# A layer-norm chain with a shorter reciprocal square root, its normalization on ScalarE, and a raised scheduling priority

## The chip, the core and the metric

One core of a Trainium2 chip runs the whole program. The metric is the device time of one execution in microseconds (us). Engines are named as in the profile: PE is TensorE (matmuls and PE transposes), DVE is VectorE, ACT is ScalarE, POOL is GpSimd, SP issues the DMAs. Each engine works through its own list of instructions in order.

## What is computed

256 tokens of width 1024 pass through 12 sublayers (4 layers of feed-forward, mixer, feed-forward; the mixers are latent attention, differential attention, a Mamba-2 scan and latent attention again), each closed by a residual sum and a layer norm, and then through a second block of three sublayers with RMS norms. What the change touches is the closing of a sublayer:

```python
def _layernorm(x, g, b):
    xf = x.astype(jnp.float32)
    mu = jnp.mean(xf, axis=-1, keepdims=True)
    var = jnp.mean(jnp.square(xf - mu), axis=-1, keepdims=True)
    return ((xf - mu) * lax.rsqrt(var + LN_EPS) * g + b).astype(x.dtype)

def _rmsnorm(x, g):
    xf = x.astype(jnp.float32)
    return (xf * lax.rsqrt(jnp.mean(xf * xf, axis=-1, keepdims=True) + RMS_EPS) * g).astype(x.dtype)

def _swiglu(h, w_in, w_out):
    gate, up = jnp.split(h @ w_in, 2, axis=-1)
    return (jax.nn.silu(gate) * up) @ w_out

def _sublayer(x, fn, mod_j, g, b, weight):
    shift, scale, gate = mod_j[:, 0, None, :], mod_j[:, 1, None, :], mod_j[:, 2, None, :]
    y = fn(x * (1 + scale) + shift)
    return _layernorm(DEEPNORM_ALPHA * x + weight * gate * y, g, b)
```

Weights and activations are float32.

## The kernel before, in words

**Tiles.** The tokens are two tiles of 128 rows, t = 0 and t = 1. A product of float32 operands is made of three matmuls of rounded parts (`mm3`, lines 252 to 254): high activation by high weight, high by low, low by high. So each weight that a DMA brings in (`raw`) is split: ACT copies the high part (`whi`, line 219, 128x1024 at a time) and DVE subtracts to get the low part (`wlo`, line 222, pieces of 384, 384 and 256 columns). These splits run all the time beside the matmuls, and most of DVE's and ACT's instructions are of this kind.

**A feed-forward (FFN).** 11 blocks of the hidden width. For each block and tile `first` makes `hid` (lines 252 to 254), ACT the gate `sg` (line 613), DVE the product `ac` (line 616); `turn` transposes `ac` on PE (line 263) and splits the result into `ah` (ACT, line 625) and `al` (DVE, line 626); `second` adds to the output banks `y` with three matmuls (line 640 `whi` by `ah`, 641 `wlo` by `ah`, 642 `whi` by `al`). In PSUM, `y0q` belongs to tile 0 and `y1q` to tile 1. Near its end the steps stand in the order `O1.b T1.c F O1.c D1` after `D0`: tile 0 is closed (`D0`) while tile 1 still has blocks to do, and then tile 1 (`D1`).

**The close of a sublayer.** `post_ln` (line 521), called once for each tile of the 12 sublayers, 24 times in all: on DVE y times gate (528) and plus ALPHA times x (529) for two halves of 512, `bn_stats` (530), `bn_aggr` (532), the reciprocal root `rstd` (311 to 325, three Newton steps on a 128x1 column, with alternating lines 319 and 320), and the normalization of `r` in two halves of 512 (535). Then `halves` transposes `r` on PE in two groups of four (`tr<-k_ident,r`, line 263), ACT applies gain, bias and modulation during the evacuation (`ev`, line 285) and takes the high part (`tmp`, line 287), and DVE the low part (295). That is what the next sublayer's first matmul (`hid0t`, `pa` or `ph`) waits for. The plain output `x = r*lng + lnb` (540, 541, full width) is a `late` step that only the next close needs.

**rstd elsewhere.** 62 calls: 24 from layer norms, 30 more for a single column (RMS norms, among them `cn`, line 768, of the latent attention, and the end of the kernel, line 589), 8 for several columns, which use lines 322 to 324.

**What sets the order.** Strings such as the one quoted list the steps of a sublayer. Within it the framework's scheduler sorts each engine's instructions by priority (by default the order of writing) as their inputs are expected to be ready, and fills gaps between dependent instructions with others, so `wlo` pieces stand between the steps of a layer norm.

Of the kernel before, what the change touches and what calls it, by code (L numbers as in the profile page):

```python
# [13 lines left out]
I32 = mybir.dt.int32  # L14
AF = mybir.ActivationFunctionType
OP = mybir.AluOpType
# [15 lines left out]
WLO, ACH, WHI, NRM = 384, 1024, 1024, 512  # L32
# [131 lines left out]
class Net:  # L164
# [145 lines left out]

    def rstd(self, var, n, mul, eps):
        e = self.nc.vector
        v, h, r, t = (self.small(n, z) for z in ("rv", "rh", "rs", "rt"))
        e.tensor_scalar(v, var, mul, eps, op0=OP.mult, op1=OP.add)
        e.tensor_scalar(r.bitcast(I32), v.bitcast(I32), -0.5, 1597463007.0, op0=OP.mult, op1=OP.add)
        e.tensor_scalar(h, v, -0.5, None, op0=OP.mult)
        for _ in range(3):
            if n == 1:
                e.tensor_scalar(t, h, r, r, op0=OP.mult, op1=OP.mult)
                e.tensor_scalar(r, t, 1.5, r, op0=OP.add, op1=OP.mult)  # L320
            else:
                e.tensor_tensor(t, r, r, OP.mult)
                e.tensor_tensor(t, t, h, OP.mult)
                e.scalar_tensor_tensor(r, t, 1.5, r, OP.add, OP.mult)
        return r

    def rms_from(self, ss, n, dim, eps=RMS_EPS):
# [193 lines left out]
    def post_ln(self, t, y, k, last=False):  # L521
        nc = self.nc
        x = self.x[t]
        r = self.tmp([P, 1024], name="r")
        st = self.small(12, "st").rearrange("p (a b) -> p a b", a=2)
        for q in range(2):
            sl = slice(q * 512, (q + 1) * 512)
            nc.vector.scalar_tensor_tensor(r[:, sl], y[q], self.gweight, self.gw[:, sl], OP.mult, OP.mult)
            nc.vector.scalar_tensor_tensor(r[:, sl], x[:, sl], ALPHA, r[:, sl], OP.mult, OP.add)
            nc.vector.bn_stats(st[:, q, :], r[:, sl])  # L530
        mv = self.small(2, "mv")
        nc.vector.bn_aggr(mv, st)
        rs = self.rstd(mv[:, 1:2], 1, 1.0, LN_EPS)
        for q in range(0, 1024, NRM):
            nc.vector.tensor_scalar(r[:, q:q + NRM], r[:, q:q + NRM], mv[:, 0:1], rs, op0=OP.subtract, op1=OP.mult)
        lng, lnb, xn = self.lng, self.lnb, self.xn
        GB = self.GB.get(k)

        def gain():
            nc.vector.tensor_tensor(x, r, lng, OP.mult)  # L540
            nc.vector.tensor_tensor(x, x, lnb, OP.add)

        if last:
            return [gain]
        if k == 3 * DEPTH:
            if GB is None:
                GB = self.GB[k] = self.small(8, "G"), self.small(8, "B")
                for o, v in zip(GB, (self.lngc, self.lnbc)):
                    nc.vector.tensor_tensor(o, v[:, (k - 1) * 8:k * 8], self.g2["pre_mix_g_2"], OP.mult)

            def late():
                gain()
                ss = self.small(2, "ss")
                self.square([x[:, q * 512:(q + 1) * 512] for q in range(2)], ss)
                self.pre_rms(t, ss)
            return self.halves(r, xn, t, GB[0], GB[1]) + [late]
        self.late.append(gain)
        return self.halves(r, xn, t, GB[0], GB[1])
# [1035 lines left out]
```

## Time and profile before

| | |
|---|---|
| three runs | 2566.07, 2568.09, 2568.38 us, median 2568.09 |
| span of the profiled execution | 2567.9 us (its own time is not listed apart from the three) |
| PE busy | 2497.5 us, 97% |
| DVE busy | 2129.1 us, 83% |
| ACT busy | 1286.9 us, 50% |
| chain that ended last | PE 86%, DVE 7%, DMA 3%, ACT 2%, issue 1% |

The busy time of an engine is a sum over all its instructions, the chain follows back from the last instruction what released each step. A row of the timeline has start, duration, engine, line, operation, output and inputs, and in brackets how long the engine had been idle and who ended that. A row for several instructions of one kind carries a count (x5).

### The profile page before, as it was taken

How to read it: one execution, taken by the hardware profiler on the slowest of the kernel's cores; microseconds unless marked ns; L12 is line 12 of the kernel's file. 1: busy time of each engine (PE TensorE's matmuls, PEld its weight loads, DVE VectorE, ACT ScalarE, POOL GpSimd, SP SyncE). 2: the span in 40 equal slices, each digit the busy share in tenths (PEclk: the TensorE clock that was granted, in tenths of full speed). 3: DMA queues.
4: the chain of work that ended last, by engine and by line, in shares of the span. 5: the costliest groups of instructions: out<-in, count | busy, mean ns of one | idle time of the engine just before them, and what ended most of it. 6: DMA issues, size and time to landing. Idle time of an engine off the chain costs nothing.

```text
span 2567.9 us, 34087 instructions
## 1 busy us (share of the span) xinstructions
PE 2497.5 (97%) x12252; PEld 2065.0 (80%) x12252; DVE 2129.1 (83%) x4847; ACT 1286.9 (50%) x2005; POOL 0.2 (0%) x4
## 2 busy tenths in 40 slices
PE   7999899999999999999999999999989999999998
PEld 6788688888887788888889778887878888788887
DVE  7888988879898988898989987698898856896754
ACT  3544474444446544544566554454446544555542
POOL 0000000000000000000000000000000000000000
PEclk9999999999999999999999999999999999999999
DMA  8888457848876388688742457658845754444552
GB/s 309 308 340 306 159 194 276 309 169 300 321 267 256 123 299 320 221 299 316 270 158 99 164 202 292 252 211 324 310 166 211 275 179 175 164 157 172 200 180 80
DMA packets 92297, 599.15 MB, mean 233 GB/s; under 512 B 12768, under 2 KB 14432, under 8 KB 24672
## 3 DMA queue, kind: packets, MB, share of 16 engines
q1 hardware_dynamic: 92128, 596.98, 63.5%
q8 instruction: 96, 1.57, 0.2%
q14 instruction: 73, 0.60, 0.1%
HBM read 593.79 MB, written 3.15 MB: 232 GB/s over the span
## 4 chain that ended last, share of the span: by engine, by line
PE 86%; DVE 7%; DMA 3%; ACT 2%; issue 1%; SPq 0%; DVEq 0%; ACTq 0%
PE tr L263 4%; PE y0q L640 3%; PE y0q L642 3%; PE y0q L641 3%; PE y1q L640 3%; PE y1q L642 3%; PE y1q L641 3%; DVE wlo L222 2%; PE hid0t L254 1%; PE hid6t L253 1%; PE hid9t L252 1%; PE hid6t L254 1%; PE hid9t L254 1%; PE hid6t L252 1%; PE hid5t L254 1%; PE hid9t L253 1%
## 5 line engine op out<-in xcount | busy, mean ns | idle before, releaser
L222 DVE TENSOR_TENSOR wlo<-raw,whi 128x384 fp32r<-128x384 f32 (+1 forms) x2385 | 1081.7, 505 | 145.8 <-ACT whi L219 76.0
L219 ACT ACTIVATE whi<-raw 128x1024 fp32r<-128x1024 f32 (+1 forms) x801 | 820.2, 1051 | 377.3 <-DMA raw<-in_ffn_w_in_dram 133.5
L371 DVE SCALAR_TENSOR_TENSOR acc<-rawm,cond,acc 128x1024 f32<-128x1024 f32 x252 | 322.9, 1281 | 13.2 <-DMA rawm<-in_w_mod_dram 8.0
L640 PE MATMUL y1q<-whi,ah 128*128 128x512 f32 x396 | 161.7, 408 | 1.7 <-ACT ah L625 1.7
L640 PE MATMUL y0q<-whi,ah 128*128 128x512 f32 x396 | 156.2, 394 | 0.7 <-ACT ah L625 0.2
L642 PE MATMUL y1q<-whi,al 128*128 128x512 f32 x396 | 156.4, 395 | 0.0
L641 PE MATMUL y0q<-wlo,ah 128*128 128x512 f32 x396 | 155.2, 392 | 0.0
L642 PE MATMUL y0q<-whi,al 128*128 128x512 f32 x396 | 155.2, 393 | 0.0
L641 PE MATMUL y1q<-wlo,ah 128*128 128x512 f32 x396 | 155.0, 391 | 0.0
L625 ACT ACTIVATE ah<-tr 128x256 fp32r<-128x256 f32 x198 | 74.7, 382 | 139.6 <-PE tr L263 136.7
L626 DVE TENSOR_TENSOR al<-tr,ah 128x256 fp32r<-128x256 f32 x198 | 82.0, 418 | 34.5 <-ACT ah L625 33.9
L640 PEld LDWEIGHTS y0q<-whi,ah 128*128 128x128 f32 x396 | 74.4, 188 | 17.1 <-ACT ah L625 2.6
L642 PEld LDWEIGHTS y1q<-whi,al 128*128 128x128 f32 x396 | 74.4, 188 | 15.7
L640 PEld LDWEIGHTS y1q<-whi,ah 128*128 128x128 f32 x396 | 74.5, 188 | 14.8 <-ACT ah L625 2.4
L642 PEld LDWEIGHTS y0q<-whi,al 128*128 128x128 f32 x396 | 74.3, 188 | 14.9 <-DVE al L626 0.2
L641 PEld LDWEIGHTS y0q<-wlo,ah 128*128 128x128 f32 x396 | 74.4, 188 | 14.5
L641 PEld LDWEIGHTS y1q<-wlo,ah 128*128 128x128 f32 x396 | 74.7, 189 | 13.2
L285 ACT ACTIVATE ev<-tr,B,G 128x128 f32<-128x128 f32 x192 | 72.9, 466 | 20.4 <-PE tr L263 20.3
L263 PEld LDWEIGHTS tr<-k_ident,ac 128*128 128x128 f32 x396 | 54.0, 140 | 29.6 <-DVE ac L616 3.0
L263 PE MATMUL tr<-k_ident,ac 128*128 128x128 f32 x396 | 74.5, 273 | 2.5 <-DVE ac L616 2.0
L295 DVE TENSOR_TENSOR tmp<-ev,tmp 128x512 fp32r<-128x512 f32 (+1 forms) x76 | 50.5, 664 | 12.7 <-ACT tmp L287 11.8
L252 PE MATMUL hid0t<-whi,tmp 128*128 128x512 f32 x144 | 56.4, 392 | 1.9 <-ACT tmp L287 1.9
(510 smaller groups left out, 6006.0 us busy)
## 6 DMA issues: line engine op xcount, KB each, us to landing
raw<-in_ffn_w_in_dram SPq DMA_DIRECT2D x176, 1024.0 KB, 4.9
rawm<-in_w_mod_dram SPq DMA_DIRECT2D x144, 1024.0 KB, 4.8
raw<-in_ffn_w_out_dram SPq DMA_DIRECT2D x88, 1024.0 KB, 5.0
raw<-in_w_gate_up_dram SPq DMA_DIRECT2D x22, 1024.0 KB, 4.7
raw<-in_w_in_dram SPq DMA_DIRECT2D x14, 1024.0 KB, 4.7
raw<-in_diff_w_in_dram SPq DMA_DIRECT2D x12, 1024.0 KB, 4.7
raw<-in_w_down_dram SPq DMA_DIRECT2D x11, 1024.0 KB, 4.7
raw<-in_w_kv_mem_dram SPq DMA_DIRECT2D x8, 1024.0 KB, 6.4
```

Of the source, the lines that this page charges most:

```text
L219: nc.scalar.activation(hi[:, q:e], s[:, q:e], AF.Copy)
L222: nc.vector.tensor_tensor(lo[:, q:e], s[:, q:e], hi[:, q:e].bitcast(F32), OP.subtract)
L252: nc.tensor.matmul(ps, xh, hi[:, off:off + n], start=first, stop=False)
L254: nc.tensor.matmul(ps, xl, hi[:, off:off + n], start=False, stop=last)
L263: self.nc.tensor.transpose(ps[:, j, :], src[:, j * P:(j + 1) * P], self.ident)
L285: nc.scalar.activation(src[:, j, :], ps[:, j, :], AF.Identity, scale=sc, bias=bcols[:, c + j:c + j + 1])
L371: nc.vector.scalar_tensor_tensor(o, src, sc, o, OP.mult, OP.add)
L625: nc.scalar.activation(ah, tr, AF.Copy)
L626: nc.vector.tensor_tensor(al, tr, ah.bitcast(F32), OP.subtract)
L640: nc.tensor.matmul(y[t][q], ah[:, k, :], hi[:, sl], start=f, stop=False)
L641: nc.tensor.matmul(y[t][q], ah[:, k, :], lo[:, sl], start=False, stop=False)
L642: nc.tensor.matmul(y[t][q], al[:, k, :], hi[:, sl], start=False, stop=l)
```

## The change

Three edits.

- **rstd**: the sum with epsilon and the halving become one instruction (h), the seed of the Newton iteration is taken with a negative sign from h, and for one column the step `t = h*r*r` is a `scalar_tensor_tensor` with one per-row pointer operand (r) in place of a `tensor_scalar` with two; `r = (t - 1.5)*r` has an immediate in place of a pointer. For several columns only the signs change and one instruction goes.
- **normalization**: two ACT instructions (Identity, 128x512, scale `rs` and bias `nb` as pointers, line 541 of the changed file) in place of two on DVE, and a new DVE instruction `nb = -mean*rs` (line 539).
- **priority**: the chain from line 528 to the normalization runs inside `tc.high_priority()`.

```diff
--- before.py
+++ after.py
@@ -310,18 +310,16 @@
 
     def rstd(self, var, n, mul, eps):
         e = self.nc.vector
-        v, h, r, t = (self.small(n, z) for z in ("rv", "rh", "rs", "rt"))
-        e.tensor_scalar(v, var, mul, eps, op0=OP.mult, op1=OP.add)
-        e.tensor_scalar(r.bitcast(I32), v.bitcast(I32), -0.5, 1597463007.0, op0=OP.mult, op1=OP.add)
-        e.tensor_scalar(h, v, -0.5, None, op0=OP.mult)
+        h, r, t = (self.small(n, z) for z in ("rh", "rs", "rt"))
+        e.tensor_scalar(h, var, 0.5 * mul, 0.5 * eps, op0=OP.mult, op1=OP.add)
+        e.tensor_scalar(r.bitcast(I32), h.bitcast(I32), -0.5, 1593268703.0 - 2147483648.0, op0=OP.mult, op1=OP.add)
         for _ in range(3):
             if n == 1:
-                e.tensor_scalar(t, h, r, r, op0=OP.mult, op1=OP.mult)
-                e.tensor_scalar(r, t, 1.5, r, op0=OP.add, op1=OP.mult)
+                e.scalar_tensor_tensor(t, r, h, r, OP.mult, OP.mult)
             else:
                 e.tensor_tensor(t, r, r, OP.mult)
                 e.tensor_tensor(t, t, h, OP.mult)
-                e.scalar_tensor_tensor(r, t, 1.5, r, OP.add, OP.mult)
+            e.scalar_tensor_tensor(r, t, 1.5, r, OP.subtract, OP.mult)
         return r
 
     def rms_from(self, ss, n, dim, eps=RMS_EPS):
@@ -522,6 +520,12 @@
         nc = self.nc
         x = self.x[t]
         r = self.tmp([P, 1024], name="r")
+        with self.tc.high_priority():
+            self.ln_chain(t, x, y, r)
+        return self.ln_rest(t, x, r, k, last)
+
+    def ln_chain(self, t, x, y, r):
+        nc = self.nc
         st = self.small(12, "st").rearrange("p (a b) -> p a b", a=2)
         for q in range(2):
             sl = slice(q * 512, (q + 1) * 512)
@@ -531,8 +535,13 @@
         mv = self.small(2, "mv")
         nc.vector.bn_aggr(mv, st)
         rs = self.rstd(mv[:, 1:2], 1, 1.0, LN_EPS)
+        nb = self.small(1, "nb")
+        nc.vector.scalar_tensor_tensor(nb, mv[:, 0:1], -1.0, rs, OP.mult, OP.mult)
         for q in range(0, 1024, NRM):
-            nc.vector.tensor_scalar(r[:, q:q + NRM], r[:, q:q + NRM], mv[:, 0:1], rs, op0=OP.subtract, op1=OP.mult)
+            nc.scalar.activation(r[:, q:q + NRM], r[:, q:q + NRM], AF.Identity, scale=rs, bias=nb)
+
+    def ln_rest(self, t, x, r, k, last):
+        nc = self.nc
         lng, lnb, xn = self.lng, self.lnb, self.xn
         GB = self.GB.get(k)
```

Line numbers behind `post_ln` grow by 9 (640 to 642 become 649 to 651, 625 becomes 634, 626 becomes 635, 540 becomes 549).

**Place 1: the end of the first layer's second FFN, tile 0.** PE, before: `ac` is the last hidden block of tile 1, `r` the normalized tile 0.

```order
L263 MATMUL tr_5287<-k_ident,ac_5273 128x128 x2
L263 MATMUL tr_5294<-k_ident,r_5221 128x128 x4
L640 MATMUL y1q_802_3879<-whi_5122,ah_5290 128x512
L641 MATMUL y1q_802_3879<-wlo_5123,ah_5290 128x512
L263 MATMUL tr_5306<-k_ident,r_5221 128x128 x4
L642 MATMUL y1q_802_3879<-whi_5122,al_5291 128x512
L640 MATMUL y1q_802_3879<-whi_5128,ah_5290 128x512
L641 MATMUL y1q_802_3879<-wlo_5129,ah_5290 128x512
L642 MATMUL y1q_802_3879<-whi_5128,al_5291 128x512
L640 MATMUL y1q_803_3880<-whi_5122,ah_5290 128x512
```

PE, now:

```order
L263 MATMUL tr_5275<-k_ident,ac_5261 128x128 x2
L263 MATMUL tr_5282<-k_ident,r_5209 128x128 x4
L649 MATMUL y1q_796_3867<-whi_5110,ah_5278 128x512
L650 MATMUL y1q_796_3867<-wlo_5111,ah_5278 128x512
L649 MATMUL y1q_797_3868<-whi_5110,ah_5278 128x512
L650 MATMUL y1q_797_3868<-wlo_5111,ah_5278 128x512
L263 MATMUL tr_5294<-k_ident,r_5209 128x128 x4
L651 MATMUL y1q_796_3867<-whi_5110,al_5279 128x512
L649 MATMUL y1q_796_3867<-whi_5116,ah_5278 128x512
L650 MATMUL y1q_796_3867<-wlo_5117,ah_5278 128x512
```

The second group of transposes of `r` has moved behind two more matmuls, and both `ah` matmuls of the first weight come before the first one with `al`.

ACT at the same place, before (`ev` and `tmp` evacuate the transposes of `r`):

```order
L219 ACTIVATE whi_5391<-raw_5383 128x1024
L219 ACTIVATE whi_5399<-raw_5397 128x1024
L625 ACTIVATE ah_5290<-tr_5287 128x256
L285 ACTIVATE ev_5299<-tr_5294,B_4284,G_4283 128x128 x4
L285 ACTIVATE ev_5311<-tr_5306,B_4284,G_4283 128x128
L287 ACTIVATE tmp_5217<-ev_5299 128x512
```

ACT, now (line 541 is the normalization):

```order
L219 ACTIVATE whi_5387<-raw_5385 128x1024
L541 ACTIVATE r_5209<-r_5209,nb_5230,rs_5220 128x512 x2
L634 ACTIVATE ah_5278<-tr_5275 128x256
L285 ACTIVATE ev_5287<-tr_5282,B_4272,G_4271 128x128 x4
L219 ACTIVATE whi_5393<-raw_5385 128x1024
L287 ACTIVATE tmp_5205<-ev_5287 128x512
```

`ah` stands behind the two normalizations, and one `whi` stands ahead of the first `tmp`.

DVE at the same place, before:

```order
L222 TENSOR_TENSOR wlo_5386<-raw_5383,whi_5385 128x256
L320 TENSOR_SCALAR rs_5233<-rt_5234,rs_5233 128x1
L222 TENSOR_TENSOR wlo_5392<-raw_5383,whi_5391 128x384
L535 TENSOR_SCALAR r_5221<-r_5221,mv_5229,rs_5233 128x512 x2
L626 TENSOR_TENSOR al_5291<-tr_5287,ah_5290 128x256
L222 TENSOR_TENSOR wlo_5392<-raw_5383,whi_5391 128x384
L222 TENSOR_TENSOR wlo_5392<-raw_5383,whi_5391 128x256
L222 TENSOR_TENSOR wlo_5400<-raw_5397,whi_5399 128x384 x2
L222 TENSOR_TENSOR wlo_5400<-raw_5397,whi_5399 128x256
L540 TENSOR_TENSOR x_507<-r_5221,lng_5213 128x1024
L295 TENSOR_TENSOR tmp_5219<-ev_5299,tmp_5217 128x512
L528 SCALAR_TENSOR_TENSOR r_5330<-y1q_802_3879,gw_4929 128x512
```

DVE, now:

```order
L322 SCALAR_TENSOR_TENSOR rs_5220<-rt_5221,rs_5220 128x1
L222 TENSOR_TENSOR wlo_5380<-raw_5371,whi_5379 128x384
L539 SCALAR_TENSOR_TENSOR nb_5230<-mv_5217,rs_5220 128x1
L222 TENSOR_TENSOR wlo_5380<-raw_5371,whi_5379 128x384
L222 TENSOR_TENSOR wlo_5380<-raw_5371,whi_5379 128x256
L222 TENSOR_TENSOR wlo_5388<-raw_5385,whi_5387 128x384 x2
L222 TENSOR_TENSOR wlo_5388<-raw_5385,whi_5387 128x256
L549 TENSOR_TENSOR x_503<-r_5209,lng_5201 128x1024
L635 TENSOR_TENSOR al_5279<-tr_5275,ah_5278 128x256
L550 TENSOR_TENSOR x_503<-x_503,lnb_5202 128x1024
```

`al` has moved behind the gain multiplication of the full width (540 before, 549 now). The ten `wlo` pieces and the `ac` that stand among the chain's steps, from line 528 to 535, stand among them still, from line 532 to 539. (At tile 0 of the two FFNs of the second layer one `wlo` piece fewer stands there than before, at the end of the differential attention one more.)

**Place 2: the end of the Mamba sublayer, tile 0.** PE, before:

```order
L252 MATMUL y1q_2839_13983<-whi_14193,half_14339 128x512
L253 MATMUL y1q_2839_13983<-wlo_14194,half_14339 128x512
L263 MATMUL tr_14399<-k_ident,r_14279 128x128 x4
L263 MATMUL tr_14411<-k_ident,r_14279 128x128 x4
L254 MATMUL y1q_2838_13982<-whi_14179,half_14340 128x512
L252 MATMUL y1q_2838_13982<-whi_14179,half_14339 128x512
```

PE, now:

```order
L252 MATMUL y1q_2822_13949<-whi_14163,half_14303 128x512
L253 MATMUL y1q_2822_13949<-wlo_14164,half_14303 128x512
L254 MATMUL y1q_2822_13949<-whi_14163,half_14304 128x512
L263 MATMUL tr_14363<-k_ident,r_14243 128x128 x4
L263 MATMUL tr_14375<-k_ident,r_14243 128x128 x4
L252 MATMUL hid0t_2940_14471<-whi_14389,tmp_14239 128x512
L253 MATMUL hid0t_2940_14471<-wlo_14390,tmp_14239 128x512
```

The eight transposes of `r` stood amid the matmuls of `y1q`, 20 of which follow them in front of `hid0t`; they now stand behind all of these and right ahead of `hid0t`.

## Rows read from the trace of the kernel before

**Rows 1.** Page, section 1 (busy time of each engine) and section 4 (the chain).
```profile
PE 2497.5 (97%) x12252; PEld 2065.0 (80%) x12252; DVE 2129.1 (83%) x4847; ACT 1286.9 (50%) x2005; POOL 0.2 (0%) x4
...
PE 86%; DVE 7%; DMA 3%; ACT 2%; issue 1%; SPq 0%; DVEq 0%; ACTq 0%
```

**Rows 2.** Waits of PE: us in total, times, longest us.
```profile
PE tr L263 <- DVE cn L768: 6.9, 2, 3.7
...
PE tr L263 <- DVE r L535: 3.4, 7, 0.9
```

**Rows 3.** Timeline of DVE at the end of an FFN: start us, us, instruction.
```profile
554.46 0.69 DVE L528 SCALAR_TENSOR_TENSOR r<-y0q,gw 128x512 f32<-128x512 f32 x1 [0.16 <-PE y0q L642]
...
560.15 0.14 DVE L316 TENSOR_SCALAR rh<-rv 128x1 f32<-128x1 f32 x1
...
560.67 0.27 DVE L319 TENSOR_SCALAR rt<-rh,rs 128x1 f32<-128x1 f32 x1
560.86 0.41 DVE L222 TENSOR_TENSOR wlo<-raw,whi 128x256 fp32r<-128x256 f32 x1
561.19 0.20 DVE L320 TENSOR_SCALAR rs<-rt,rs 128x1 f32<-128x1 f32 x1
...
563.99 1.00 DVE L535 TENSOR_SCALAR r<-r,mv,rs 128x512 f32<-128x512 f32 x2
...
565.24 2.15 DVE L222 TENSOR_TENSOR wlo<-raw,whi 128x384 fp32r<-128x384 f32 x5
567.31 1.22 DVE L540 TENSOR_TENSOR x<-r,lng 128x1024 f32<-128x1024 f32 x1
```

**Rows 4.** Timeline of ACT at the same place.
```profile
564.20 0.38 ACT L625 ACTIVATE ah<-tr 128x256 fp32r<-128x256 f32 x1 [0.66 <-PE tr L263]
```

**Rows 5.** Timeline of PE at the same place.
```profile
564.68 0.63 PE L263 MATMUL tr<-k_ident,r 128*128 128x128 f32 x4 [0.51 <-DVE r L535]
565.06 0.48 PE L640 MATMUL y1q<-whi,ah 128*128 128x512 f32 x1
...
568.34 0.39 PE L252 MATMUL hid0t<-whi,tmp 128*128 128x512 f32 x1
```

**Rows 6.** Instructions of a line: duration ns min/median/max, first and last start, forms.
```profile
L324 DVE SCALAR_TENSOR_TENSOR rs<-rt,rs x24: 142/158/165, 838.7 to 2290.7; 128x4 f32<-128x4 f32 x18, 128x8 f32<-128x8 f32 x6
...
L529 DVE SCALAR_TENSOR_TENSOR r<-x,r x48: 670/683/694, 261.3 to 2180.1; 128x512 f32<-128x512 f32 x48
...
L589 DVE SCALAR_TENSOR_TENSOR x<-r,rs,x x12: 735/746/753, 2302.9 to 2564.0; 128x512 f32<-128x512 f32 x12
...
L292 ACT ACTIVATE tmp<-ev x24: 417/623/635, 12.4 to 2386.6; 128x512 fp32r<-128x512 f32 x16, 128x256 fp32r<-128x256 f32 x4, 128x384 fp32r<-128x384 f32 x4
...
L1116 ACT ACTIVATE xs<-xs,rs x8: 707/719/727, 1351.2 to 1474.9; 128x512 f32<-128x512 f32 x8
```

**Rows 7.** Timeline of PE at four other places.
```profile
285.05 0.69 PE L263 MATMUL tr<-k_ident,cn 128*128 128x128 f32 x2 [3.67 <-DVE cn L768]
...
884.40 0.50 PE L252 MATMUL hid0t<-whi,tmp 128*128 128x512 f32 x1 [1.94 <-ACT tmp L287]
...
1490.38 1.05 PE L263 MATMUL tr<-k_ident,r 128*128 128x128 f32 x8
...
2189.46 0.50 PE L253 MATMUL ph<-wlo,tmp 128*128 128x512 f32 x1 [1.74 <-DVE wlo L222]
```

**Rows 8.** Windows: us, busy us of each engine, PEclk, DMA share, GB/s.
```profile
283.00:290.00 7.00, 4.83 (x14) 3.37 (x15) 6.58 (x25) 2.66 (x6) 0.00 (x0) 0.53 0.34 136
880.00:890.00 10.00, 8.06 (x38) 5.99 (x37) 9.79 (x20) 7.12 (x13) 0.00 (x0) 1.00 0.54 200
1345.00:1360.00 15.00, 15.00 (x128) 15.00 (x127) 14.42 (x47) 9.90 (x17) 0.00 (x0) 1.00 0.19 68
2191.00:2195.00 4.00, 3.81 (x10) 2.99 (x11) 3.93 (x15) 3.35 (x7) 0.00 (x0) 0.57 0.21 37
```

**Rows 9.** Timeline of DVE at the end of the kernel.
```profile
2563.38 1.42 DVE L589 SCALAR_TENSOR_TENSOR x<-r,rs,x 128x512 f32<-128x512 f32 x2
```

## The prediction, made before the changed kernel ran

> **What bounds the kernel now.** I began with the page. PE is busy for 97% of the span and makes 86% of the chain that ended last; DVE makes 7% of that chain and ACT 2% [rows 1]. So the end is set by the stream of matmuls plus the places where PE stands still. The change removes no matmul: it can only shorten such waits, or make new ones. Next I read PE's waits. The reader should see how little of them a layer norm owns: PE waited for the normalized `r` 7 times, 3.4 us in total, and for the `cn` of the latent attention, which stands behind a layer norm on DVE, twice, 6.9 us [rows 2]. That is 10.3 us of 2567.9, so even a chain of no length would save little more than 0.4%. Then I read the timelines at an end of an FFN [rows 3 to 5], the durations of instructions near to the new ones [rows 6], and the longest waits elsewhere with the clock around them [rows 7, 8].
>
> The sum goes against the profiled span of 2567.9 us; the median of the runs is 0.2 us above it, and I add that at the end. A difference under 0.2%, 5.1 us, counts as no change.
>
> **Shorter reciprocal root.** The merged first step saves one 128x1 instruction, 0.14 us as line 316, its like, takes [rows 3]. The new `t` has one pointer in place of two and the new `r` none in place of one. A `scalar_tensor_tensor` without pointer takes 158 ns on a short column, and a pointer adds 746 - 683 = 63 ns (lines 324, 589 and 529 in [rows 6]). So `t` falls from 0.27 to 0.22 and `r` from 0.20 to 0.16 [rows 3]; three steps save 0.29, and a call 0.43 by durations. But an instruction starts before the one ahead has ended (the `wlo` at 560.86, while line 319 runs to 560.94 [rows 3]), so each removed one is worth about 0.08 less and the saving is 0.37 where DVE is full. I take 0.37. The Trainium skill ("VectorE: DVE Perf Modes", section "The DRAIN you can't avoid") says that the next instruction does not start until the pipe has emptied. By that the saving would be 0.43, and the sum below some 0.4 us lower at six places; the starts in this trace do overlap, so I don't take it.
>
> **Normalization on ACT.** On DVE the pair took 1.00 us (line 535 in [rows 3]). Nothing in the trace has this form with two pointers. The nearest rows are 623 ns without and 719 ns with one, both 128x512 (lines 292 and 1116 in [rows 6]); a second pointer at the same 96 ns gives 0.81. Below, it might cost nothing (0.72), above, twice that (0.91). I take 0.81, 1.5 us for the pair with some overlap (1.3 to 1.8). `nb` is new, one pointer, 0.22 us on DVE, and the step to ACT some 0.07. So the chain to the end of `r` loses 0.37 and gains about 0.8.
>
> **Priority.** The order shows that the chain is not drawn together: it still has ten `wlo` pieces among its steps at place 1, because each step waits for the one ahead and DVE's gap is filled. I cost it at nothing by itself; what it moves is in the next terms.
>
> **What is queued behind, place 1.** This is the largest term. Before, ACT had been idle 0.66 us when it made `ah` at 564.20, with 0.38 us [rows 4], and PE's first matmul with it started at 565.06, behind the transposes of `r` at 564.68 [rows 5]. Now `ah` stands behind the two normalizations. The chain began at 554.46 and reached the normalization at 563.99 [rows 3]; with the same pieces among it `nb` starts at 563.99 - 0.37 = 563.62, ACT starts at 563.9, ends the pair at 565.4 and `ah` at 565.75. PE's first matmul moves to 565.8, **0.76 later**. The first transposes need only the first half of `r` (564.7), so they add nothing. By the order this happens at six ends of an FFN, tile 0 (layer 1 second, layer 2 both, layer 3 second, layer 4 both). At two of them a `wlo` piece fewer stands in the chain, about 0.4 us, so 0.35 is left. 4 x 0.76 + 2 x 0.35 = **+3.7**.
>
> `al` now stands behind the gain multiplication. From `nb`, five pieces (2.07 us from 565.24 to 567.31 [rows 3]) and the multiplication (about 1.15 of its 1.22) put its start at 563.62 + 0.14 + 2.07 + 1.15 = 566.98 and its end at 567.4. The order puts four matmuls and four transposes ahead of the first one that needs it. From 565.06 to 568.34 stand twelve matmuls and four transposes [rows 5], so a matmul takes about 0.24 and the transposes 0.37; PE is there at 565.8 + 4 x 0.24 + 0.37 = 567.1 and waits some 0.4. Six such places: **+2.4**; if the DVE work in front is quicker, nothing.
>
> **Place 2.** The transposes of `r` at the Mamba's end started at 1490.38 [rows 7], and twenty matmuls covered their evacuation. Now they stand right ahead of `hid0t`, as they do already at the end of the differential attention, where `hid0t` waited 1.94 us [rows 7]. So **+1.9**. At that other place itself the chain gains 0.8 - 0.37 and one `wlo` piece: **+0.7**, uncovered.
>
> **Where it gains.** `cn` waits 3.7 and 3.2 us [rows 2]. Its root and the layer norm's stand on DVE together, with no gap left for fillers; two roots less 0.37 each and the pair of 1.00 gone from DVE make up to 1.7 each; the order moves other pieces in between, so I take 0.8 each for tile 0 and as much for tile 1: **-3.2** (0 to -5). After that wait PE's granted clock was 0.53, its lower level of 1.2 GHz, between 283 and 290 [rows 8], and 14 matmuls and transposes ran in 4.83 us there; at the 0.24 us of place 1 they would take 3.4. I expect one of the two stretches to stay full: **-1.4**. The hybrid's start has a wait of 1.74 us for a `wlo` piece [rows 7] that the order now puts ahead of the gains, less the longer pair: **-1.2**. The Mamba's eight roots save 8 x 0.37 = 3.0 of DVE, but PE was busy for all of 15 us around them, from 1345 us on [rows 8]: I take **-1.0**. The last root ends the kernel's chain ahead of line 589 [rows 9], uncovered: **-0.4**. The 48 normalizations free 24 us of DVE for the splits; covered by matmuls but for **-0.5**.
>
> **The clock.** New waits can drop the clock. After 1.74 us at 2189.46 it was 0.57; after 1.94 us at 884.40 it stayed 1.00 [rows 7, 8]. So a wait of that length may or may not do it. Ten pieces ran in the 4 us from 2191 to 2195 [rows 8], which at 0.24 take 2.4: a drop costs about 1.6. I put in one: **+1.7**.
>
> **Sum.** +3.7 + 2.4 + 1.9 + 0.7 + 1.7 = +10.4 of cost; -3.2 - 1.4 - 1.2 - 1.0 - 0.4 - 0.5 = -7.7 of gain. +2.7 on 2567.9 is 2570.6, and with the 0.2 to the median **2570.8 us**.
>
> **Rivals.**
> *A, slower: ACT's queue.* `ah`, the normalization and the evacuation stand in one line on ACT. If the pair takes 1.8 and the `whi` ahead of `tmp` holds the next sublayer's first matmul too, PE's standstill at a place 1, which is 0.51 now [rows 5], becomes 0.51 + 0.76 + 0.4 and more, past the 1.7 from which a clock drop has been seen. Five such drops of 1.6 us in place of one add 6.5: 2577 us, and 2574 to 2582 with three to eight. For it: one drop was seen after 1.74 [rows 7, 8]. Against: the standstill there is in three pieces, not in one. The Trainium skill ("TensorE: Matmul & The Clock Gate", Part 1) holds that an idle array goes to the slow clock and a busy one leaves it; the trace agrees for the 3.67 us wait [rows 7, 8], and 884 shows that a shorter one need not.
> *B, faster: DVE's relief.* The pieces that DVE does sooner close the waits for `ah` and `al`, and only the gains, place 2 and the differential attention's end are left: -7.7 - 1.4 (the second stretch of the clock) + 1.9 + 0.7 = -6.5, or 2561.5; with `cn` at its bound of -5, 2559.7. I put it at 2560.5. For it: ACT is busy for only half of the span [rows 1]. Against: the order itself puts `ah` behind the pair.
> *C: the change doesn't do what it says.* The chain stays as interleaved as it was, what it saves is filled by `wlo` pieces, and the waits are absorbed by neighbours: 2567 to 2569.
>
> **How the numbers follow.** Forecast 0.46 (its own range 2565 to 2576), A 0.24, B 0.18, C 0.12. Above 2573.2 are 0.22 of A and 0.07 of the forecast's upper part: slower 0.29. Below 2563 are B and 0.02 of the forecast's lower part: faster 0.20. Within 0.2%: 0.51. From 2559 to 2580 about 0.08 is left out at each end.
>
> **What would show it.** Right: in the new trace's waits, line 649 waits for `ah` (line 634) at six places by 0.5 to 1 us, line 651 for `al`; `hid0t` at the Mamba's end waits about 2 us; line 541 takes 0.8 each and line 535 is gone; the waits for `cn` are shorter. A: granted clock under 1.00 in windows behind the FFN ends. B: no wait for `ah`, and full clock in both stretches behind `cn`. Wrong altogether: PE waits that are new at places not named here, for a `wlo` or a `whi` that came late, as the splits are moved at every close.

## The result and the profile after

The changed kernel took **2583.11 us** (median; runs from 2579.68 to 2584.79), the kernel before 2567.08 us beside it (2564.69 to 2568.38): a ratio of **1.0062 [1.0048, 1.0076]**, 16 us more. By 2% that is the same time; by the 0.2% that the prediction's chances go by it is slower. The forecast, 2570.8, was too low, and the range, to 2580, ended below the median. The profiled execution has a span of 2577.9 us and a time of 2579.68, the shortest of the four. With the same 1.8 us around the span, the trace of before (2567.9 us) was an execution of some 2569.7 us.

The page after, sections 1 and 4, against [rows 1]:

```profile
PE 2501.4 (97%) x12252; PEld 2064.3 (80%) x12252; DVE 2095.9 (81%) x4761; ACT 1324.6 (51%) x2055; POOL 0.2 (0%) x4
...
PE 87%; DVE 8%; ACT 3%; DMA 2%; issue 1%; SPq 0%; DVEq 0%; ACTq 0%
```

DVE lost 33 us of work, ACT gained 38, and the kernel became slower: how much work an engine has did not decide, but what waits for it and when. PE's waits after (us in total, times, longest), against [rows 2]:

```profile
PE tr L263 <- DVE cn L777: 4.8, 2, 2.6
...
PE hid0t L252 <- ACT tmp L287: 3.8, 2, 2.1
PE tr L263 <- ACT r L541: 3.5, 7, 0.8
PE y1q L649 <- ACT ah L634: 3.0, 9, 0.5
PE tr L263 <- ACT ev L285: 2.9, 7, 1.6
...
PE px L1021 <- DVE cacc L1014: 2.1, 1, 2.1
```

The same three products in the trace of before:

```profile
PE hid0t L252 <- ACT tmp L287: 1.9, 1, 1.9
PE y1q L640 <- ACT ah L625: 1.7, 3, 0.7
PE tr L263 <- ACT ev L285: 1.2, 1, 1.2
```

The wait for `cn` is 2.1 us shorter than in this trace, the one for `r` unchanged. `ah` now holds PE nine times in place of three, the evacuation `ev` seven times in place of once. The second wait of `hid0t` is new, and so is that of `px` (a product of the Mamba).

**The end of an FFN**, the same place as [rows 3 to 5]. DVE, ACT and PE (start us, us, instruction):

```profile
558.75 0.69 DVE L532 SCALAR_TENSOR_TENSOR r<-y0q,gw 128x512 f32<-128x512 f32 x1 [0.15 <-PE y0q L651]
...
567.92 0.15 DVE L539 SCALAR_TENSOR_TENSOR nb<-mv,rs 128x1 f32<-128x1 f32 x1
567.99 2.16 DVE L222 TENSOR_TENSOR wlo<-raw,whi 128x384 fp32r<-128x384 f32 x5
570.07 1.21 DVE L549 TENSOR_TENSOR x<-r,lng 128x1024 f32<-128x1024 f32 x1
571.20 0.41 DVE L635 TENSOR_TENSOR al<-tr,ah 128x256 fp32r<-128x256 f32 x1
```

```profile
568.11 1.52 ACT L541 ACTIVATE r<-r,nb,rs 128x512 f32<-128x512 f32 x2 [1.22 <-DVE nb L539]
569.53 0.36 ACT L634 ACTIVATE ah<-tr 128x256 fp32r<-128x256 f32 x1
569.80 1.49 ACT L285 ACTIVATE ev<-tr,B,G 128x128 f32<-128x128 f32 x4
```

```profile
568.97 0.66 PE L263 MATMUL tr<-k_ident,r 128*128 128x128 f32 x4 [0.51 <-ACT r L541]
569.95 0.50 PE L649 MATMUL y1q<-whi,ah 128*128 128x512 f32 x1 [0.32 <-ACT ah L634]
...
571.35 0.66 PE L263 MATMUL tr<-k_ident,r 128*128 128x128 f32 x4 [0.21 <-ACT ev L285]
...
573.69 0.39 PE L252 MATMUL hid0t<-whi,tmp 128*128 128x512 f32 x1
```

ACT stands idle for 1.22 us until `nb` comes, then does the two normalizations, and only then `ah`. From the first transposes of `r` to `hid0t` PE now takes 4.72 us (568.97 to 573.69), before 3.66 (564.68 to 568.34 [rows 5]), with the same eight transposes and twelve matmuls: **+1.06 us** here. The first matmul with `ah` comes 0.60 us later, counted from the chain's first instruction (569.95 - 558.75 against 565.06 - 554.46). `al` holds nobody; the second four transposes wait for `ev`, which stands behind the same pair on ACT.

**The Mamba's end**, ACT, then PE, against 1490.38 in [rows 7]:

```profile
1500.00 1.51 ACT L541 ACTIVATE r<-r,nb,rs 128x512 f32<-128x512 f32 x2
```

```profile
1504.81 1.04 PE L263 MATMUL tr<-k_ident,r 128*128 128x128 f32 x8
1507.93 0.71 PE L252 MATMUL hid0t<-whi,tmp 128*128 128x512 f32 x1 [2.09 <-ACT tmp L287]
1508.44 0.63 PE L253 MATMUL hid0t<-wlo,tmp 128*128 128x512 f32 x1
```

`r` was complete at 1501.5, but its transposes are written 3.3 us later, right ahead of `hid0t`. So `hid0t` waits 2.09 us, and the matmuls behind it run at the lower clock, as the last of these windows shows (us, busy us of each engine, granted clock, DMA share, GB/s; the first is the FFN's end, the second the `px` of the Mamba):

```profile
569.00:574.00 5.00, 4.47 (x22) 3.33 (x23) 5.00 (x9) 5.00 (x12) 0.00 (x0) 1.00 0.68 267
1361.00:1369.00 8.00, 5.88 (x37) 5.71 (x36) 7.51 (x23) 5.12 (x9) 0.00 (x0) 0.79 0.68 255
1508.00:1512.00 4.00, 4.00 (x11) 3.17 (x12) 4.00 (x15) 3.95 (x7) 0.00 (x0) 0.57 0.42 113
```

The normalization itself, line 541 (duration ns min/median/max) and what ACT sat idle for ahead of it:

```profile
L541 ACT ACTIVATE r<-r,nb,rs x48: 797/802/817, 270.7 to 2200.4; 128x512 f32<-128x512 f32 x48
its engine sat idle before it (us, times) until:
  DVE nb L539: 18.8, 18
```

### The profile page after: what moved, and what is told of

Same layout as the page of the kernel before. It is cut to its first block, busy times and chain, and to the rows that moved or that the text cites. A ratio compares the mean times of both kernels' runs of the same rounds, so it can differ in the third digit from the quotient of the medians.

```text
span 2577.9 us, 34067 instructions
## 1 busy us (share of the span) xinstructions
PE 2501.4 (97%) x12252; PEld 2064.3 (80%) x12252; DVE 2095.9 (81%) x4761; ACT 1324.6 (51%) x2055; POOL 0.2 (0%) x4
## 4 chain that ended last, share of the span: by engine, by line
PE 87%; DVE 8%; ACT 3%; DMA 2%; issue 1%; SPq 0%; DVEq 0%; ACTq 0%
PE tr L263 4%; PE y0q L649 3%; PE y0q L651 3%; PE y0q L650 3%; PE y1q L651 3%; PE y1q L649 3%; PE y1q L650 3%; DVE wlo L222 3%; PE hid0t L254 1%; PE hid0t L252 1%; PE hid0t L253 1%; PE hid6t L253 1%; PE hid1t L252 1%; PE hid9t L254 1%; PE hid9t L252 1%; PE hid8t L252 1%
```

## The experiments

Three theories had to be told apart. **Queue** (Q): the pair on ACT is longer and stands in front of `ah`, `ev` and `tmp`; undoing the edit on ACT gives the time back. **Lateness** ("latency" in the expectations): undoing that edit helps too, but because `r` itself is complete later, behind `nb` and the longer pair. **Order** (P for the priority, S for any change): the raised priority or the shorter root re-sorts the splits and transposes elsewhere; undoing that gives the time back. Ratios are to the kernel before on the same chip, with a 95% interval.

### Each edit alone, and two by two

`e1_rstd`, the root alone:

```diff
-        e.tensor_scalar(v, var, mul, eps, op0=OP.mult, op1=OP.add)
...
-        e.tensor_scalar(h, v, -0.5, None, op0=OP.mult)
+        e.tensor_scalar(h, var, 0.5 * mul, 0.5 * eps, op0=OP.mult, op1=OP.add)
...
-                e.tensor_scalar(t, h, r, r, op0=OP.mult, op1=OP.mult)
+                e.scalar_tensor_tensor(t, r, h, r, OP.mult, OP.mult)
```

> The kernel before with the shorter reciprocal root alone: normalization on DVE, no raised priority. Theory Q (the loss of some 16 us comes from the normalization standing in ScalarE's queue ahead of ah and the evacuations): 3 us faster to no change, 2564 to 2567 us. Theory P (it comes from the raised priority, which moves gains, transposes and splits of the neighbouring steps): the same, 2564 to 2567. Theory S (the scheduler re-sorts all that stands near a chain whenever one of its instructions changes, and any new order is worse than the old one): 3 to 8 us slower, 2570 to 2575.

`e2_act`, the normalization on ACT alone:

```diff
+        nb = self.small(1, "nb")
+        nc.vector.scalar_tensor_tensor(nb, mv[:, 0:1], -1.0, rs, OP.mult, OP.mult)
-            nc.vector.tensor_scalar(r[:, q:q + NRM], r[:, q:q + NRM], mv[:, 0:1], rs, op0=OP.subtract, op1=OP.mult)
+            nc.scalar.activation(r[:, q:q + NRM], r[:, q:q + NRM], AF.Identity, scale=rs, bias=nb)
```

> The kernel before with the normalization on ScalarE alone: old reciprocal root, no raised priority. Its ScalarE order puts the two normalizations ahead of ah at five of the six FFN ends named in the prediction. Theory Q: 12 to 22 us slower, 2579 to 2589 us, since the chain is longer by nb and a root that was not shortened; ah waits of 0.7 to 1.2 us at these ends. Theory P: 0 to 5 us slower. Theory S: 3 to 8 us slower.

`e3_pri`, the priority alone:

```diff
+        with self.tc.high_priority():
+            self.ln_chain(t, x, y, r)
+        return self.ln_rest(t, x, r, k, last)
```

> The kernel before with the raised priority alone: old reciprocal root, normalization on DVE. Theory Q: within 4 us of before, 2563 to 2571. Theory P: 8 to 16 us slower, 2575 to 2583, with new waits of PE at the start of the sublayers that follow. Theory S: 3 to 8 us slower.

`e4_rstd_pri` has the diffs of `e1_rstd` and `e3_pri`, `e6_rstd_act` those of `e1_rstd` and `e2_act`, `e7_act_pri` those of `e2_act` and `e3_pri`:

> The changed kernel without its second edit: shorter root and raised priority, normalization left on DVE. Theory Q: 2560 to 2567 us, no slower than before, so the whole loss is gone. Theory P: 2574 to 2583. Theory S: 2570 to 2577.

> The changed kernel without the raised priority. If the costs of the normalization on ScalarE (16 us alone) and of the priority (8 us alone) lie at different places and add up, then the changed kernel, at 16 us, must hold a gain from the root in this company, and this one is 8 us faster than it, 2573 to 2577 us. If the two overlap (the longer chain hides what the priority moves), it is no faster: 2578 to 2584.

> The changed kernel with the old reciprocal root. If the costs add up: 16 + 8 = 24 us slower than before, 2586 to 2593 us. If they overlap: 2579 to 2585 us.

| kernel | median us (runs) | ratio to before |
|---|---|---|
| root | 2567.47 (11) | 1.0003 [0.9994, 1.0013] |
| ACT | 2581.93 (5) | 1.0062 [1.0049, 1.0075] |
| priority | 2573.96 (10) | 1.0033 [1.0022, 1.0044] |
| root, priority | 2574.21 (6) | 1.0035 [1.0021, 1.0048] |
| root, ACT | 2578.18 (7) | 1.0050 [1.0033, 1.0067] |
| ACT, priority | 2583.46 (4) | 1.0071 [1.0045, 1.0097] |
| all three | 2583.11 (4) | 1.0062 [1.0048, 1.0076] |

The root costs and saves nothing. ACT alone makes as much as the whole change, priority alone half as much, and the two do not add. So the edit on ACT has the larger part, by the queue or by lateness, and the order theory is not empty. PE's waits with the root and ACT, without priority:

```profile
PE hid0t L252 <- ACT tmp L287: 3.8, 2, 2.1
...
PE tr L263 <- ACT r L540: 3.6, 6, 0.8
PE y1q L648 <- ACT ah L633: 3.0, 9, 0.5
PE tr L263 <- ACT ev L285: 2.7, 7, 1.6
```

They are the waits of the changed kernel, and with ACT alone they stand there too (3.8, 5.5, 3.3 and 3.3 us): none of them comes from the priority.

That the root saves nothing is told by its own waits. With it alone, PE waits for `r` twice, 0.8 us, in place of 7 times, 3.4 us [rows 2]. But the order is sorted anew in the mixers, and this is new:

```profile
1360.24 0.36 PE L1018 MATMUL px<-tmp,whi 128*128 128x256 f32 x1 [2.12 <-DVE cacc L1011]
```

The same 2.1 us stand in every kernel here with the short root and in none with the old one, and the two waits of `po` for `pT` (latent attention) grew from 0.6 to 2.1 us. PE's idle time over the whole trace came to 174.9 us against 173.4 in the second trace of before. (It is summed here from start to start of neighbouring matmuls, less the 20th percentile of that distance for the first one's shape; lower clock is in it.)

### Before and after once more, and where the time goes by stages

`e5_before`, `e13_after`, `e14_after` and `e16_pri` have no edit of their own: they are further executions, traced.

> The kernel before once more, for a second trace of it. The runs of one kernel spread by 5 us either way, and the trace that the prediction used may have been one of the slower ones. If that is so, the new span lies 2 to 6 us below 2567.9 us; if its waits at the layer norms are steady, those at the six FFN ends are the same to 0.05 us and the difference lies in the first 136 us and in stretches of the lower clock.

> The changed kernel once more, for a second trace: its first one was its fastest run, 2579.7 us where the median is 2583.1. If the rest of the loss lies in some place that the first trace does not show, a run of 2582 us and more has it at one or two sublayers, as extra waits of PE there of 2 us and more against the first trace. If it is scattered (stretches of the lower clock that come or go, the weights at the start), every sublayer is within 0.5 us of the first trace and the difference lies in the first 136 us and in the number of such stretches.

> The changed kernel a third time, with the same question as the second trace of it.

> The raised priority alone once more. Its median was 8 us over the kernel before, its trace 5.6 over the second trace of that. If the loss is a place, it is at the same sublayers in both traces; if it is scattered, the sublayers differ between the two.

They took 2567.55 (before), 2577.60 and 2575.17 (after) and 2569.23 us (priority); the last three ran on one chip, where an execution of before took 2569.63 us. Here is how much later (us) the middle of each FFN comes than in `e5_before`, worked out from the starts of the same products `ac` in both traces (to some 0.3 us). Latent attention lies between F1 and F2 and between F7 and F8, differential attention between F3 and F4, the Mamba between F5 and F6; F9 is the second block's.

| trace | F1 | F2 | F3 | F4 | F5 | F6 | F7 | F8 | F9 |
|---|---|---|---|---|---|---|---|---|---|
| before, first trace | -0.9 | -1.0 | -0.8 | -1.9 | -2.0 | -0.5 | 1.6 | 2.0 | 2.0 |
| root | 0.6 | 3.2 | 4.0 | 3.1 | 3.5 | 3.1 | 3.1 | 2.6 | 0.2 |
| priority | -0.3 | 1.4 | 2.2 | 3.1 | 4.3 | 4.9 | 5.6 | 5.5 | 5.6 |
| priority, second | -1.0 | 0.5 | 1.3 | 1.8 | 2.8 | 2.0 | 2.4 | 3.1 | 1.7 |
| ACT | -0.5 | 0.3 | 3.6 | 5.1 | 6.5 | 12.8 | 14.3 | 15.9 | 14.0 |
| root, ACT | -0.2 | 0.9 | 3.0 | 3.4 | 4.6 | 10.7 | 12.0 | 12.3 | 10.9 |
| after, first | 1.1 | 3.3 | 4.9 | 6.4 | 7.5 | 12.7 | 13.9 | 13.8 | 12.5 |
| after, second | -1.6 | -0.4 | 1.3 | 2.1 | 3.2 | 8.4 | 9.8 | 9.8 | 10.4 |
| after, third | -0.3 | 1.1 | 2.8 | 3.4 | 4.5 | 8.0 | 9.4 | 9.0 | 7.9 |
| split (last experiment) | 1.0 | 1.3 | 2.2 | 0.6 | 1.1 | 2.2 | 2.8 | 2.3 | 0.1 |

From F5 to F6, over the Mamba, 3.5 to 6.3 us are added in the rows with the whole pair on ACT, under 1 with root or priority alone, 1.1 with the split, and 1.5 between the two traces of before. Each step from an FFN straight to the next adds 1 to 3 more. Elsewhere traces of one kernel differ nearly as much as the kernels do. The new order on ACT also brings two more `ACT_TABLE_LOAD` of 1.28 us, both in the Mamba (29 in the trace after, 27 before); they do not explain its step, since the kernel with the priority alone has 29 as well. The second execution with the priority shows nothing: 2569.23 us beside 2569.63 for before. Its cost in the timed runs is not tied to any place.

### The queue by itself

`e8_dummy` keeps the normalization on DVE, with the root, and adds two ACT instructions of the same shape whose output nothing reads; that is work beyond the reference's.

```diff
+        for q in range(0, 1024, NRM):
+            junk = self.half([P, NRM], name="sq")
+            nc.scalar.activation(junk, self.lng[:, q:q + NRM], AF.Identity, scale=rs, bias=nb)
```

> The kernel with the shorter root alone (normalization on DVE, no raised priority), to which each layer norm adds nb and two ScalarE instructions of the same form and size as the normalization, 128x512 with two pointers, whose output nobody reads (they read the gain row). So r comes as early as with the root alone, and ScalarE's queue is as full as in the changed kernel. Theory Q1 (the cost is the queue: ah and the evacuations stand behind the pair): 8 to 16 us slower than before, with waits for ah of 0.3 us and more at the FFN ends. Theory Q2 (the cost is the latency: r itself comes later, by the longer pair and the step from DVE to ScalarE): 0 to 4 us slower, the ah waits there but small.

2620.89 us (4 runs), 1.0220 [1.0194, 1.0246]: far more than the pair itself. ACT's timeline shows where:

```profile
1533.26 1.52 ACT L543 ACTIVATE sq<-lng,nb,rs 128x512 f32<-128x512 f32 x2 [4.48 <-DVE nb L538]
1534.68 1.83 ACT L285 ACTIVATE ev<-tr,B,G 128x128 f32<-128x128 f32 x5
```

As nobody waits for them, the order places them where ACT then stands for 4.48 us until `nb` is there, and the evacuation that `hid0t` needs stands behind; PE waits 9.6 us for it there. Over the trace ACT stands 60.5 us ahead of these instructions until `nb` comes, and 41.1 us are lost to the lower clock, against 16.0 in the second trace of before, so about half of the loss is clock. As a price of the queue the run is spoiled; it shows what one instruction that waits at the head of an in-order engine does.

`e9_ah_first`: as `e6_rstd_act`, with raised priority for `ah` and `al` of tile 1's last block. In the trace `ah` then stands between the two normalizations of an FFN's end, no longer behind both.

```diff
+            if b == NB - 1 and t == 1:
+                with self.tc.high_priority():
+                    nc.scalar.activation(ah, tr, AF.Copy)
+                    nc.vector.tensor_tensor(al, tr, ah.bitcast(F32), OP.subtract)
```

> Shorter root and normalization on ScalarE without raised priority (2578.2 us), and now ah and al of the last hidden block of tile 1 get the raised priority instead: on ScalarE ah then stands between the two normalizations or ahead of them at six of the seven FFN ends. Queue theory (ah behind the pair holds PE): the waits for ah at these ends fall from 0.5 us to under 0.2, and the kernel gains 2 to 5 us, 2573 to 2576. Latency theory (r itself is late, and whatever stands in front of the second half is paid back in the transposes): the transposes of r wait longer by what ah no longer does, 2577 to 2580 us.

> The kernel with ah ahead of the pair once more: its trace gained 0.75 us at each of five FFN ends against its base, but its median of 2582 us did not (base 2578.2). If the gain at these ends is real, this trace shows 1.0 us of waits there again (base 1.7), and the loss against the base lies elsewhere, at a place that can be named.

2582.19 us (5), 1.0051 [1.0032, 1.0070], and 2580.19 in `e15_ah_first`, one execution of the same kernel. At the FFN's end of [rows 3 to 5] PE takes 3.84 us from the first transposes of `r` to `hid0t`, in place of 4.71 in `e6_rstd_act` (3.66 before), and nothing of it is in the time. Both expected ranges, 2573 to 2576 for the queue and 2577 to 2580 for lateness, lie below the median. `e10_tr_first` (to `e6_rstd_act`) and `e12_root_tr` (to `e1_rstd`) raise the transposes of `r` instead:

```diff
+            with self.tc.high_priority():
+                self.to_pair(src, n, dst, t, gcols=gcols, bcols=bcols, a0=a0)
```

> The same base (2578.2 us) with raised priority for the transposes of r and their evacuation. At the Mamba's end the eight transposes now stand twelve and more matmuls ahead of hid0t in place of right ahead of it. If the place of the transposes there costs what the trace of the changed kernel shows (2.3 us of waiting for tmp and a stretch of the lower clock of 1.7 us), that end is 3 to 4 us shorter than in the base, against at most 1 us lost at each FFN end, where ah now stands behind four evacuations: 2572 to 2582 us in all, with the Mamba end's stage 3 us and more below the base. If it is the longer chain and not the place, that stage stays within 1 us of the base.

> A try at a better version: shorter root, normalization on DVE, no raised priority for the chain, but for the transposes of r and their evacuation. The waits at the ends of the mixers (2 us for hid0t behind the differential attention, 2 us at the hybrid's start) may shrink by up to 1 us each, the FFN ends lose up to 0.4 each where ah stands behind evacuations: 2562 to 2570 us.

2605.44 us (5), 1.0161 [1.0136, 1.0186], and 2587.37 (5), 1.0076 [1.0056, 1.0095]. Both are slower than expected, by 23 and 17 us beyond the upper bound. In the first the Mamba's end was mended (`hid0t` waits 0.20 us in place of 2.08), but elsewhere the transposes now stood so early that PE waited for the evacuation. Its wait:

```profile
PE tr L263 <- ACT ev L285: 26.1, 17, 3.1
```

`e17_mended` is `e9_ah_first` with the transposes raised at the Mamba's end alone:

```diff
+        if k == 8 and t == 0:
+            def first(f):
+                with self.tc.high_priority():
+                    f()
+            return [lambda f=f: first(f) for f in hs]
```

> Shorter root and the whole normalization on ScalarE without raised priority for the chain (2578.2 us), with both of its named costs taken away: ah of the last hidden block of tile 1 ahead of or between the normalizations, and the transposes of r at the Mamba's end, tile 0, given priority so that they stand amid the matmuls of y1q. If these two places carry the loss of 11 us, its trace shows at the Mamba's end under 1 us of waits (base 4.0) and 1.0 at the FFN ends (base 1.7), and the time is 2567 to 2573 us. If the move to ScalarE costs in some other way, it stays at 2575 us and above.

2578.80 us (5), 1.0050 [1.0033, 1.0066]. PE at the Mamba's end:

```profile
1502.08 0.60 PE L263 MATMUL tr<-k_ident,r 128*128 128x128 f32 x4
...
1507.20 0.50 PE L252 MATMUL hid0t<-whi,tmp 128*128 128x512 f32 x1 [0.19 <-ACT tmp L287]
```

Both places are mended, and the kernel is no faster than `e6_rstd_act`. So the theory that these two places alone carry the loss falls. Its trace still stands 11.3 us behind at F8, and PE's idle time is 185.7 us. Of the 11.8 us to the kernel of the next section (173.9) at most 3.0 are lower clock (14.9 us lost against 12.0). Outside of it PE stands 3.2 us longer ahead of `hid0t`, 3.0 ahead of `pmv` (at the program's start, and no longer than before the change), 1.8 ahead of the transposes of `cn`, 1.6 ahead of those of `r` and 1.4 ahead of `ph`, the second block's first product, which waits 2.18 us for `tmp` in place of 0.87. Part of it the edit makes itself: behind the second FFN of the second layer `hid0t` waits 0.70 us, where it did not wait in `e6_rstd_act`.

### The pair split over two engines

`e11_split` is the root with the first half of `r` on DVE and the second on ACT; `e18_split_pri` adds the priority.

```diff
+        nc.scalar.activation(r[:, 512:], r[:, 512:], AF.Identity, scale=rs, bias=nb)
+        nc.vector.tensor_scalar(r[:, :512], r[:, :512], mv[:, 0:1], rs, op0=OP.subtract, op1=OP.mult)
```

> Shorter root, no raised priority, first half of r normalized on DVE and the second on ScalarE. Queue theory: half the ScalarE time stands in front of ah, so about half of the loss of the full move (11 us): 2570 to 2574 us. Latency theory: r is complete no later than with DVE alone, so no loss: 2564 to 2569.

> The changed kernel with all three edits, but only the second half of r normalized on ScalarE and the first on DVE. Here the second group of transposes at the Mamba's end still stands right ahead of hid0t. If what remains is the cost of the raised priority as with DVE alone (8 us), 2573 to 2577 us; if the place at the Mamba's end comes on top (2 to 4 us), 2576 to 2580; if half a pair on ScalarE costs nothing and the priority nothing either, 2565 to 2570.

The split took 2567.47 us (11), **1.0002 [0.9993, 1.0012]**; with priority 2571.17 (11), 1.0015 [1.0006, 1.0024]. DVE and ACT at the FFN's end, split without priority:

```profile
565.77 0.15 DVE L538 SCALAR_TENSOR_TENSOR nb<-mv,rs 128x1 f32<-128x1 f32 x1
565.84 0.54 DVE L540 TENSOR_SCALAR r<-r,mv,rs 128x512 f32<-128x512 f32 x1
```

```profile
565.96 0.82 ACT L539 ACTIVATE r<-r,nb,rs 128x512 f32<-128x512 f32 x1 [1.22 <-DVE nb L538]
566.68 0.36 ACT L633 ACTIVATE ah<-tr 128x256 fp32r<-128x256 f32 x1
```

The halves run beside each other. PE can begin after DVE's 0.54 us (it does so 9.92 us after the chain's first instruction, not 10.22), and `ah` starts 0.72 us after ACT's part begins, not 1.42 (568.11 to 569.53). PE's waits:

```profile
PE tr L263 <- DVE r L540: 1.6, 6, 0.5
```

The waits for `ah` are back at those of the root alone as well (0.9 us, twice). With half of the work still on ACT the loss is gone, so what costs is the whole pair there, not that ACT does it. Why it costs, the split does not decide, because it shortens two things at once: what stands in front of `ah` and `ev`, and the time until `r` is complete. At the FFN's end shown, `r` was complete 10.53 us after the chain's first instruction before and 10.88 us after. The expectation gave 2570 to 2574 us by the queue and 2564 to 2569 by lateness. The time fits lateness, the gain at the FFN's end with `ah` moved fits the queue, and the two are not told apart here.

Where PE stands because of the pair, all traces together show. Outside the lower clock its idle time is 160 to 164 us in the four traces of before, root and split, 163 to 167 in the four with the priority besides, and 168 to 175 in the nine with the whole pair on ACT (`e10_tr_first` left out). The last lie 10.6 us above the first on average: 4.0 ahead of the transposes of `r`, 3.9 ahead of `hid0t`, 2.0 ahead of `y1q`, and 0.7 in all elsewhere. The lower clock takes as much in one group as in the other.

With this split the priority costs 3.7 us (2571.17 less 2567.47), under the 0.2%; the two were timed on different chips, their intervals overlap a little, and 2571.17 lies in none of the ranges expected for it. No kernel here is faster than before.

## Why the prediction was wrong

**Right: the terms of place 1.** "`nb` starts at 563.99 - 0.37" made 9.16 us from the chain's first instruction; it was 9.17 (558.75 to 567.92). 0.81 us each was 0.80, `nb` 0.15 in place of 0.22. The largest term, "0.76 later" for `ah` and "some 0.4" for `al`, 1.16 at a full place, came to 1.06, though `ah` gave 0.60 of it and the rest was a wait for `ev`, not `al`. The six ends together, from the chain's first instruction to the next sublayer's first product, grew by 5.1 us where +3.7 and +2.4 were put. (By the prediction's own figures three steps of the root save 0.27 and a call 0.35 us, not 0.29 and 0.37; that changes nothing here.) "The first transposes need only the first half of r, so they add nothing" held at this place: the wait is 0.51 as before [rows 5].

**Right: place 2 and the differential attention's end.** From the chain's first instruction to `hid0t` the Mamba's end grew from 17.01 to 18.92 us, the +1.9 of the sum; behind it came a stretch of the lower clock in two of three traces. The prediction had one drop, but for no place. The differential attention's end, priced at +0.7, grew from 14.61 to 15.16 us.

**Wrong: the gains.** This is the step that failed: the -7.7 hardly came. The root alone, from which much of it was to come, saves nothing (1.0003 [0.9994, 1.0013]). `cn` saved 2.1 us against the first trace of before and 0.6 against the second, where -3.2 was put, and the latent attention's stage of layer 1 was no earlier (F1 to F2 adds 1.2 to 2.2 us). To the lower clock, where -1.4 was put behind `cn`, the whole trace after lost 16.1 us (length times the missing clock, summed; 11.8 and 16.3 in the other two), the two of before 19.3 and 16.0. "I take -1.0" for the Mamba's roots became +2.1 at `px`: with the shorter root the neighbours are sorted anew, which the prediction saw for the priority ("what it moves is in the next terms") and not for the root. The second block's start did gain 1.1 to 1.3 in two of three traces (F8 to F9). Leaving the gains out, +10.4 on the span is 2578.3, and some 2 us more as a time: near to the changed kernel's traced executions (2575.2 to 2579.7) and 3 us under its median.

**Wrong: "I cost it at nothing by itself".** Priority alone is 1.0033 [1.0022, 1.0044], some 8 us, in ten runs, and some 4 us on top of the split. Its place I did not find.

**Wrong: the baseline.** "The median of the runs is 0.2 us above" took span for time. With 1.8 us around the span, the trace was 2 to 4 us slower than the medians of before (2565.8 to 2567.7) measured beside the kernels above.

**Rival A** gave the right side and nearly the size, with the same queue behind it. But its size came from clock drops behind the FFN ends, and these did not come: the granted clock from 569 to 574 us is 1.00 in the windows above, and no stretch of the lower clock in the three traces lies at an FFN's end. So its size was luck. **Rivals B and C** fall with the interval.

**Open.** The later timed runs of the changed kernel (2582 to 2585) lie above all three of its traced ones; before shows no such gap. The second and third traced ones are 8.0 and 5.5 us above before on their chip, not 16, in single executions. Queue and lateness are not told apart. Why `e17_mended` wins nothing is placed only in part, and nothing tells where the priority's few microseconds are.

## What to carry to other kernels

An engine that is busy for half of the time is no free place: ask what stands behind the moved work in that engine's line at that moment, and when its result is complete. Try to split a latency chain over two engines side by side before moving it whole. Where a scheduler sorts by readiness, a shorter instruction moves its neighbours too, and here gains of a microsecond at named places were given back at unnamed ones: count on little of them, and time each edit alone. Compare with two or three traces of the same kernel before an effect of 2 or 3 us is put down to a place.

## What was not expected of the hardware

Whether the lower clock comes differs between executions of one kernel. Behind the same 2.1 us wait for `hid0t` at the Mamba's end the changed kernel lost its clock in two of three traces and kept it in the third. Between kernels it is the same: after a 2.12 us wait at `px` the one with the root alone kept its clock, and the changed kernel, after 2.1 us for the same product, did not. Windows of the first, then of the split kernel around the same place:

```profile
1355.00:1370.00 15.00, 12.62 (x101) 11.98 (x101) 14.99 (x48) 9.99 (x13) 0.00 (x0) 1.00 0.39 141
```

```profile
1360.00:1367.00 7.00, 6.94 (x58) 6.63 (x56) 7.00 (x21) 4.35 (x6) 0.00 (x0) 1.00 0.44 147
```

against 0.79 above. Most such stretches cost 1.7 us of full clock, some twice that, as from 283 to 290 us in [rows 8]; two traces of one kernel (`e9_ah_first`, `e15_ah_first`; spans 2573.8 and 2578.3) differ by 7.3 us of them (11.4 and 18.8). The Trainium skill ("TensorE: Matmul & The Clock Gate", Part 1) says of the start of a kernel that how many matmuls run slow varies from run to run; in the midst of this one the traces show the like. By its rule that an idle array falls to the slow clock, the waits of about 2 us are a place where it may fall, and the traces show both outcomes.
